# A decoder block on one core: parts of weights' sums one tile later, branch weights asked for ahead of pooling data, a table loaded earlier, and four last products on GpSimd

## The chip, the core and the metric

The kernel runs on one core of one Trainium2 chip. The core has five engines with a queue of instructions each, in order: TensorE (PE in the profile; its loads of stationary operands are listed apart as PEld), VectorE (DVE), ScalarE (ACT), GpSimd (POOL) and SyncE (SP), which here only asks for transfers. Engines wait for each other on semaphores. The metric is device time in microseconds (us), lower is better; it is compared as the median of several runs.

## What is computed

One decoder layer over a sequence of 1024 rows of width 1024, in float32:

```python
h = x
h = h + 0.5 * swiglu(rms_norm(h, ffn1_norm), ffn1_w1, ffn1_w3, ffn1_w2)     # FFN 1, inner width 2816
u = rms_norm(h, mix_norm)
proj = u @ w_in              # q | k | v of 12 heads, pooling input (512 wide), logits of two gates
gates = sigmoid(...)
y_attn = dilated_mixture_attention(q, k, v) @ w_branch_attn                  # 256 -> 1024
y_pool = multiscale_pool(pz, pool_w, pool_scale) @ w_branch_pool             # 512 -> 1024
h = h + (gates[0] * y_attn + gates[1] * y_pool) @ w_out
h = h + 0.5 * swiglu(rms_norm(h, ffn2_norm), ffn2_w1, ffn2_w3, ffn2_w2)     # FFN 2
out = rms_norm(h, final_norm)
```

where `swiglu(x, w1, w3, w2)` is `(silu(x @ w1) * (x @ w3)) @ w2` and `rms_norm` divides each row by the root of its mean square and multiplies by a gain.

## The kernel before

**Products.** Every float32 operand is split into a high part (an ACT copy to the type fp32r) and a low part (the operand less its high part, on DVE or POOL), and a product of two operands is three matmuls: high by high, high by low, low by high. The large products also use a scheme with seven block products in place of eight: 2x2 blocks of weights and of rows are added and subtracted first (tiles whose names begin with `s_` for weights; `t1` to `t4`, `b11`, `b21`, `b22` for rows), and the seven products are made of these sums. `Quad.operand(m)` (from L331) makes the weights' operand of product m: for m = 6 and m = 7 it computes sums on DVE (L345 and L347 for m = 6), then calls `Sevens.split`, which makes the high part on ACT (L303) and the low part on an engine that it is given or that it picks by a counter: every third on DVE, the others on POOL (L306).

**Entries.** Three phases begin with an entry: FFN 1, the input projection ("mix"), and FFN 2. `Entry.run` goes over the last four of the eight tiles of 128 rows, `t` = 4 to 7. For each it normalises the next tile's rows (`squares`, `inverse` with a power on POOL, `scaled` on DVE, L267), forms the row sums in PSUM with transposes on PE (L381, L458), and makes high (ACT, L382 and L398) and low parts (DVE, L385 and L401). In between PE runs two products of the first quads for each tile, and `out` empties their PSUM bank: an ACT activation, L527 in FFN 1 and FFN 2 (tile `y_f`), L1032 in the mix phase (`y_m`). At `t` = 5, behind the rest of the tile, it calls `more(0)`, which makes the operand of the first product of the main loop behind the entry (product 6 of the first quad; the text calls this operand M0); `more(1)` stands in the last tile. The order of the instructions on each engine is the order of these calls: it is written out by hand (`manual_schedule`), no scheduler changes it. Bank after bank is used in turn, so a product waits until the bank that it takes has been emptied.

**Branch data.** The inputs of the branch stage are asked for from SP's queue towards the end of the mix phase. `load_pool` (L1241) loads the pooling rows into tiles that held row sums (`xhi_b_mix`, `xlo_b_mix`, `xhi_t_mix`, `xlo_t_mix`); `load_branch` (L1243) loads the branch weights for one block (`wab`, from the DRAM tensor `late_w`, L1245) and then the gate's values for it (`gb`, L1246); `load_values` (L1234) loads v. A "ring" of tiles for q and k is filled by further DMAs (L1204, L1205) and split (L1213 on ACT, L1214 on POOL). The branch products are `yp` (L1701) and the attention's are `s`, `tp` and `o`. `end_branches` asks for the next block's branch weights when one is done.

**The output projection** (from L1999) is a loop over steps `i`; ACT makes the high part `o_hi` at L1923, PE multiplies at L1940. Behind it, FFN 2's entry uses Silu for the first time since the attention's exponentials, so ACT loads a table of functions (`ACT_TABLE_LOAD`, L531).

**The last stage** is FFN 2's down projection: steps 0 to 41, each with operands `a` (gated values, split into `ahi_f` and `alo_f`, L718 and L722) and `b` (weights, sums at L738, split into `bhi_f`, `blo_f`), with products at L760 and additions into `h_last` at L765. Every fourth low part goes to POOL except in the last two steps. Rows 4 to 7 are finished in two halves of columns: behind the addition of the low half `low_half` (L2101) squares it on ACT, and when the last of the four is done `low_rows` (L2107, L2109) multiplies all four low halves by the final gain on DVE. Behind the addition of a high half come its squares (L2113), the sum (L2117), the power on POOL (L2118), the product of the high half (L2123), the scaling of the low half (L2126) and the two stores.

Of the kernel before, what the change touches and what calls it, by code (L numbers as in the profile page):

```python
# [126 lines left out]
def tile_block(  # L127
# [191 lines left out]
    class Quad:  # L319


        def __init__(self, sv, n):
            self.sv, self.n = sv, n
            self.a = []
            self.bank, self.w = {}, {}

# [3 lines left out]

        def operand(self, m, eng=None):  # L331
            if not self.a or (m not in (1, 2) and len(self.a) == 2):
                self.get()
# [20 lines left out]
            else:  # L354
                src = half_tile("s", f"{n}4")
                ve.tensor_tensor(src, a12, self.s2, op=OP.subtract)
            self.w[m] = self.sv.split(src, f"{n}{m}", eng)

# [44 lines left out]
    class Entry:  # L403
# [18 lines left out]
        def run(self, high, after, first=0):  # L422
# [11 lines left out]
            for t in range(4, NT):  # L434
# [24 lines left out]
                if not last:  # L459
# [13 lines left out]
                    self.out(k)  # L473
                    r4 = fourth()
                    r4.lower()
                else:
# [16 lines left out]
                if t == NT - 3:  # L493
                    self.more(0)

# [349 lines left out]
    def pre_run(sv, todo, first, low):  # L845
        return Entry(sv, [(*((q.A, m, q.a_out), (q.B, m, q.b_out))[k],) for q, m in todo for k in range(2)], low,
                     lambda n: first.A.operand((6, 7)[n]))

# [394 lines left out]
    def load_branch(d):  # L1243
        w, gb = row_part(f"wab{d}"), row(f"gb{d}")
        nc.sync.dma_start(w.rearrange("p (q c) -> p q c", q=2).bitcast(F32), late_w[1 + d][:, :, 256:768])  # L1245
        nc.sync.dma_start(gb, gate_dram[d][:, 1])  # L1246
        pool_in[d] = (w.rearrange("p (q c) -> p q c", q=2), gb)

# [5 lines left out]

    def mix_operand(k):
        if k < len(items):
            q, m = items[k]
            if q == len(mixes):
                mixes.append(Mix(svm, q))
            mixes[q].quad.operand(m, None if k > 1 else gp)  # L1260

# [98 lines left out]
    with tc.manual_schedule():  # L1360
# [4 lines left out]
        for k in range(len(items) + 4):  # L1365
# [27 lines left out]
            if k == len(items) - 12:  # L1393
                later.append([k, first_ring()])
            if k == len(items) - 6:
                load_pool(2, "b11", 0)
                load_pool(3, "b11", 1)
# [3 lines left out]
            if k == len(items) - 4:  # L1401
                load_branch(0)
                load_values(0, row_part)
# [285 lines left out]
    def branch(n):  # L1689

        d, half = divmod(n, 2)
        cols = slice(half * HALF, (half + 1) * HALF)
        w, gb = pool_in[d]
        p = bank("acc", f"yp{n}")
# [14 lines left out]
    def end_branches():  # L1709
        while ends:  # L1710
            n, p = ends.pop(0)
            d, half = divmod(n, 2)
            gb = pool_in[d][1]
            cols = slice(half * HALF, (half + 1) * HALF)
            ve.tensor_tensor(gb[:, cols], p, gb[:, cols], op=OP.mult)
            if half == 1:
                stores.append((by_pool[d], gb))
                del pool_in[d]
                if d + 2 < KT:
                    load_branch(d + 2)  # L1720

    def send():
# [76 lines left out]
    with tc.manual_schedule():  # L1799
        load_ring(uses[1], ring_place(1))  # L1800
        load_branch(1)
        factors = [make_factors(hp, eng) for hp, eng in enumerate((gp, ve))]
        combines = [[combine(hp, half, adds, lower) for half in range(2)]
# [168 lines left out]
    with tc.manual_schedule():  # L1972
# [28 lines left out]
        for i in range(2, STEPS - 4):  # L2001
# [3 lines left out]
            if i in (6, 7):  # L2005
                load_whole(i + 4)
            sum_o(i + 3)
            split_o(i + 2)
# [92 lines left out]
    def low_half(t):  # L2101
# [3 lines left out]
        ends[t] = y, st  # L2105

    def low_rows(t):  # L2107
        y, _ = ends[t]
        ve.tensor_tensor(y[:, LOWS], h[t][:, LOWS], final_gain[:, LOWS], op=OP.mult)  # L2109

# [18 lines left out]
    def after2(m, t):  # L2129
# [3 lines left out]
        elif m == len(DOWN) - 2:  # L2133
            low_half(4 + t)
            if t == 3:
                for u in range(4, NT):
                    low_rows(u)
        elif m == len(DOWN) - 1:
# [103 lines left out]
```

## Time and profile before

| | |
|---|---|
| three runs | 1941.24, 1938.65, 1936.98 us; median 1938.65 us |
| profiled execution | 1938.52 us, of which the span of instructions is 1936.7 us |
| mean granted TensorE clock | 0.995 of full |
| busy: PE / DVE / ACT / POOL | 1900.9 / 1341.3 / 776.9 / 730.0 us |
| DMA traffic | 333.56 MB, mean 172 GB/s |

All times in rows are counted from the start of the span. A row of the timeline gives the start, the busy time, the engine, the line of the kernel, the operation, the output tile and its inputs, the shapes, a count when equal instructions follow each other, and in brackets the idle time of the engine just before it, with what ended it. A row of the list of waits gives total idle time, number of times and the longest one, for a pair of waiting and releasing lines. Matmuls are pipelined: each lasts 389 ns in the trace, but they follow each other more closely than that.

### The profile page before, as it was taken

The numbers are of one execution on the slowest core, as the hardware profiler recorded it, in microseconds if no ns is written. First come the engines' busy times: TensorE is split into PE (matmuls) and PEld (weight loads), VectorE is DVE, ScalarE is ACT, GpSimd is POOL, SyncE is SP. The second block draws the span as 40 slices with busy tenths as digits, with TensorE's granted clock in tenths as the row PEclk, the third lists the DMA queues.
The fourth block names the chain that finished last, engine by engine and source line by source line (L and its number), as shares of the span: only waits on it lengthen the run. The fifth ranks groups of instructions, "written<-read, shape, count | busy, mean of one in ns | idle before, by whom it ended". The sixth has DMA issues, their size and how long they took to land. (4 is left out here: it accounts for less than half of the span.)

```text
span 1936.7 us, 24862 instructions
## 1 busy us (share of the span) xinstructions
PE 1900.9 (98%) x8842; PEld 1567.9 (81%) x8842; DVE 1341.3 (69%) x2015; ACT 776.9 (40%) x1396; POOL 730.0 (38%) x556
## 2 busy tenths in 40 slices
PE   9999999999999999999999999999999999999998
PEld 7788888887888877888877888877888888878886
DVE  6786556657776776667875886878666556577777
ACT  6323333333345542334444763263333333333344
POOL 4333333332222344444544365644333333322132
PEclk9999999999999999999999999999999999999999
DMA  4164222336466626765568997642533223454564
GB/s 186 39 201 153 103 87 104 136 111 209 147 229 216 201 83 224 240 227 179 214 240 297 269 256 260 246 174 87 198 105 128 93 87 104 143 195 146 191 217 163
DMA packets 147436, 333.56 MB, mean 172 GB/s; under 512 B 20208, under 2 KB 40944, under 8 KB 145776
## 3 DMA queue, kind: packets, MB, share of 16 engines
q1 hardware_dynamic: 138096, 307.22, 47.1%
q10 hardware_dynamic: 9216, 24.75, 3.6%
q8 instruction: 70, 1.15, 0.3%
q14 instruction: 54, 0.44, 0.1%
HBM read 229.61 MB, written 102.30 MB: 171 GB/s over the span
## 5 line engine op out<-in xcount | busy, mean ns | idle before, releaser
L760 PE MATMUL d_f<-bhi_f,alo_f 128*128 128x512 f32 x616 | 240.4, 390 | 1.7 <-POOL alo_f L722 1.4
L760 PE MATMUL d_f<-bhi_f,ahi_f 128*128 128x512 f32 x616 | 240.5, 390 | 0.5 <-ACT h L389 0.5
L760 PE MATMUL d_f<-blo_f,ahi_f 128*128 128x512 f32 x616 | 239.7, 389 | 0.0
L722 POOL TENSOR_TENSOR alo_f<-g_f,ahi_f 128x512 fp32r<-128x512 f32 x68 | 96.8, 1440 | 282.7 <-ACT ahi_f L718 276.1
L314 PE MATMUL u_mixm<-xhi_t_mix,wc_mixm 128*128 128x512 f32 x608 | 195.1, 391 | 1.2 <-POOL wc_mixm L306 1.1
L314 PE MATMUL u_mixm<-xhi_b_mix,wc_mixm 128*128 128x512 f32 x456 | 148.9, 393 | 4.8 <-ACT y_m L1032 2.8
L760 PEld LDWEIGHTS d_f<-bhi_f,alo_f 128*128 128x128 f32 x616 | 115.6, 188 | 27.5 <-POOL alo_f L722 2.5
L760 PEld LDWEIGHTS d_f<-bhi_f,ahi_f 128*128 128x128 f32 x616 | 115.6, 188 | 24.6 <-ACT h L389 0.9
L314 PEld LDWEIGHTS u_mixm<-xhi_t_mix,wc_mixm 128*128 128x128 f32 x608 | 113.7, 188 | 26.5 <-POOL wc_mixm L306 3.3
L760 PEld LDWEIGHTS d_f<-blo_f,ahi_f 128*128 128x128 f32 x616 | 115.6, 188 | 23.9
L314 PE MATMUL u_mixm<-xlo_t_mix,wc_mixm 128*128 128x512 f32 x304 | 118.3, 389 | 0.0
L306 POOL TENSOR_TENSOR wc_mixm<-s_mixm,wc_mixm 128x512 fp32r<-128x512 f32 x52 | 75.2, 1447 | 107.7 <-ACT wc_mixm L303 99.7
L314 PEld LDWEIGHTS u_mixm<-xhi_b_mix,wc_mixm 128*128 128x128 f32 x456 | 85.5, 188 | 24.5 <-ACT y_m L1032 3.2
L303 ACT ACTIVATE wc_mixm<-s_mixm 128x512 fp32r<-128x512 f32 x76 | 47.7, 629 | 128.0 <-DVE s_mixm L347 53.5
L314 PE MATMUL u_mixm<-xlo_b_mix,wc_mixm 128*128 128x512 f32 x228 | 88.8, 389 | 0.0
L718 ACT ACTIVATE ahi_f<-g_f 128x1024 fp32r<-128x1024 f32 x84 | 81.8, 974 | 3.2 <-DMA g_f<-gs_f 3.2
L306 POOL TENSOR_TENSOR wc_mixm<-raw,wc_mixm 128x512 fp32r<-128x512 f32 x40 | 57.3, 1434 | 58.3 <-ACT wc_mixm L303 58.2
L1940 PE MATMUL wo<-w_o,o_hi 128*128 128x512 f32 x224 | 69.5, 391 | 0.5 <-ACT h_again L389 0.3
L718 ACT ACTIVATE bhi_f<-s_f2w 128x512 fp32r<-128x512 f32 x55 | 32.8, 627 | 88.5 <-DVE s_f2w L738 80.8
L314 PEld LDWEIGHTS u_mixm<-xlo_t_mix,wc_mixm 128*128 128x128 f32 x304 | 57.1, 188 | 11.8
L718 ACT ACTIVATE bhi_f<-s_f1w 128x512 fp32r<-128x512 f32 x55 | 33.0, 630 | 81.6 <-DVE s_f1w L738 76.7
L722 DVE TENSOR_TENSOR alo_f<-g_f,ahi_f 128x1024 fp32r<-128x1024 f32 (+1 forms) x44 | 52.7, 1198 | 7.3 <-ACT ahi_f L718 7.3
(1330 smaller groups left out, 5098.5 us busy)
## 6 DMA issues: line engine op xcount, KB each, us to landing
g_f<-gs_f SPq DMA_DIRECT2D x70, 512.0 KB, 4.5
gs_f<-y_f SPq DMA_DIRECT2D x88, 256.0 KB, 2.5
raw<-in_w2a_dram SPq DMA_DIRECT2D x35, 512.0 KB, 4.3
raw<-in_w2b_dram SPq DMA_DIRECT2D x35, 512.0 KB, 4.1
gs_f<-gb_f SPq DMA_DIRECT2D x46, 256.0 KB, 2.3
raw<-in_w1a_dram SPq DMA_DIRECT2D x22, 512.0 KB, 4.8
raw<-in_w3a_dram SPq DMA_DIRECT2D x22, 512.0 KB, 6.1
raw<-in_w1b_dram SPq DMA_DIRECT2D x22, 512.0 KB, 4.5
```

The costliest lines, as they stand in the source:

```text
L303: ac.activation(w[:, 0], src, AF.Copy)
L306: eng.tensor_tensor(w[:, 1], src, w[:, 0].bitcast(F32), op=OP.subtract)
L314: pe.matmul(p, a, b, start=(start and k == 0 and q == 0), stop=(k == 3 and q == 2), skip_group_check=not start)
L718: ac.activation(hi[:, c], src, AF.Copy)
L722: eng.tensor_tensor(lo[:, d], src[:, o], hi[:, d].bitcast(F32), op=OP.subtract)
L760: pe.matmul(self.banks[m][t], l, r, start=(first and q == 0), stop=(last and q == 2))
L1940: pe.matmul(banks[m][t], l, r, start=(st == 0 and j == 0 and q == 0), stop=(st == 1 and j == 1 and q == 2))
```

## The change

- **Entries.** `operand` is cut in two. `summed(m)` makes the sums alone (the instructions on DVE), and `operand` calls it and then splits. At `t` = 5 the entry now calls `more(0, True)`, which makes M0's sums only; the split is called at `t` = 6, between the high part of that tile's fourth sum and its low part. All three entries do so.
- **Branch weights.** The gate's load is taken out of `load_branch` into `load_gate`. For the first block the weights are now asked for ahead of the four pooling loads; the gate's values stay where they were. The other blocks keep their order.
- **Gate's table.** In the output projection's loop at `i` = 7 a one-column activation with Silu is added, so that the table is loaded there; the load at the entry of FFN 2 goes.
- **Last products.** Each low half's product with the final gain is issued on POOL (`gp`) right behind that half's squares, in `low_half`; `low_rows` and its loop go.

PE's order of instructions is the same in both kernels.

```diff
@@ Quad
         def operand(self, m, eng=None):
+            self.summed(m)
+            self.w[m] = self.sv.split(self.src.pop(m), f"{self.n}{m}", eng)
+
+        def summed(self, m):
+            if m in self.src:
+                return
             if not self.a or (m not in (1, 2) and len(self.a) == 2):
                 self.get()
...
-            self.w[m] = self.sv.split(src, f"{n}{m}", eng)
+            self.src[m] = src
@@ Entry.run
                     r4 = fourth()
+                    if t == NT - 2:
+                        self.more(0)
                     r4.lower()
...
                 if t == NT - 3:
-                    self.more(0)
+                    self.more(0, True)
@@ pre_run
-                     lambda n: first.A.operand((6, 7)[n]))
+                     lambda n, early=False: (first.A.summed if early else first.A.operand)((6, 7)[n]))
@@ mix_operand
-        mixes[q].quad.operand(m, None if k > 1 else gp)
+            if early:
+                mixes[q].quad.summed(m)
+            else:
+                mixes[q].quad.operand(m, None if k > 1 else gp)
@@ load_branch
+    def load_gate(d):
+        gb = row(f"gb{d}")
         nc.sync.dma_start(gb, gate_dram[d][:, 1])
-        pool_in[d] = (w.rearrange("p (q c) -> p q c", q=2), gb)
+        pool_in[d].append(gb)
@@ the mix phase's last items
             if k == len(items) - 6:
+                load_branch(0)
                 load_pool(2, "b11", 0)
                 load_pool(3, "b11", 1)
             if k == len(items) - 5:
                 load_pool(0, "t2", 0)
                 load_pool(1, "t2", 1)
             if k == len(items) - 4:
-                load_branch(0)
+                load_gate(0)
                 load_values(0, row_part)
@@ the output projection's loop
+            if i == 7:
+                ac.activation(warm, mhalf, AF.Silu)
             sum_o(i + 3)
             split_o(i + 2)
@@ the end
         ac.activation(y[:, LOWS], h[t][:, LOWS], AF.Square, scale=D ** -0.5, accum_out=st[:, 0:1])
         ends[t] = y, st
-
-    def low_rows(t):
-        y, _ = ends[t]
-        ve.tensor_tensor(y[:, LOWS], h[t][:, LOWS], final_gain[:, LOWS], op=OP.mult)
+        gp.tensor_tensor(y[:, LOWS], h[t][:, LOWS], final_gain[:, LOWS], op=OP.mult)
...
             low_half(4 + t)
-            if t == 3:
-                for u in range(4, NT):
-                    low_rows(u)
```

More of the change, by code (lines that the diff above doesn't have):

```diff
@@ L324, in __init__ @@
             self.a = []
-            self.bank, self.w = {}, {}
+            self.bank, self.w, self.src = {}, {}, {}
         def get(self):
@@ L1243, in load_branch @@
     def load_branch(d):
-        w, gb = row_part(f"wab{d}"), row(f"gb{d}")
-        nc.sync.dma_start(w.rearrange("p (q c) -> p q c", q=2).bitcast(F32), late_w[1 + d][:, :, 256:768])
+        w = row_part(f"wab{d}").rearrange("p (q c) -> p q c", q=2)
+        nc.sync.dma_start(w.bitcast(F32), late_w[1 + d][:, :, 256:768])
+        pool_in[d] = [w]
+    def load_gate(d):
+        gb = row(f"gb{d}")
         nc.sync.dma_start(gb, gate_dram[d][:, 1])
-        pool_in[d] = (w.rearrange("p (q c) -> p q c", q=2), gb)
+        pool_in[d].append(gb)
     mix_stack = ExitStack()
@@ L1253, in tile_block, with mix_operand @@
     items = [(q, m) for q in range(len(MIX)) for m in ORDER if q >= AHEAD or m not in (1, 2)]
-    def mix_operand(k):
+    def mix_operand(k, early=False):
         if k < len(items):
@@ L1692, in branch @@
         cols = slice(half * HALF, (half + 1) * HALF)
-        w, gb = pool_in[d]
+        w = pool_in[d][0]
         p = bank("acc", f"yp{n}")
@@ L1720, in end_branches @@
                     load_branch(d + 2)
+                    load_gate(d + 2)
     def send():
@@ L1801, in tile_block @@
         load_branch(1)
+        load_gate(1)
         factors = [make_factors(hp, eng) for hp, eng in enumerate((gp, ve))]
```

## The prediction

> **What bounds the kernel now.** I read the engine table of the page first, then the list of waits of the matrix engine (TensorE, "PE"), then the table of clock windows.
>
> ```profile
> span 1936.7 us, 24862 instructions
> PE 1900.9 (98%) x8842; PEld 1567.9 (81%) x8842; DVE 1341.3 (69%) x2015; ACT 776.9 (40%) x1396; POOL 730.0 (38%) x556
> ```
>
> TensorE is idle for 1936.7 − 1900.9 = 35.8 us of the whole span. Nothing in the change removes a matmul, so it can only win a part of these 35.8 us, or shorten stretches that ran at half clock. The list of waits says where they are (columns: who waited, for whom, us in total, times, longest):
>
> ```profile
> PE yp L1701 <- DMA wab<-late_w: 3.3, 1, 3.3
> PE u_f12a L314 <- ACT y_f L527: 3.3, 1, 3.3
> PE u_mixm L314 <- ACT y_m L1032: 2.8, 1, 2.8
> PE u_f21a L314 <- ACT y_f L527: 2.3, 1, 2.3
> PE x_t L381 <- POOL s_f2t L430: 1.2, 1, 1.2
> PE x_t L381 <- POOL s_mixt L430: 0.9, 1, 0.9
> PE x_b L381 <- DVE xlo_t_mix L401: 0.6, 1, 0.6
> ```
>
> These seven, 14.4 us, are the places that the first three parts touch. The next view has one row for each clock window (start and end; then its length, busy us of PE, PEld, DVE, ACT, POOL; the granted clock; the DMA share; GB/s):
>
> ```profile
> 48.75:52.17 3.42, 1.14 (x6) 0.60 (x4) 2.30 (x5) 2.31 (x7) 1.46 (x2) 1.00 0.01 2
> 52.17:55.58 3.41, 2.43 (x6) 1.92 (x7) 3.41 (x5) 1.58 (x4) 3.41 (x3) 0.50 0.00 0
> 55.58:58.99 3.41, 3.41 (x11) 2.63 (x10) 2.50 (x4) 1.54 (x3) 1.60 (x2) 0.50 0.45 154
> 687.04:690.46 3.42, 1.52 (x7) 0.94 (x5) 2.29 (x5) 2.27 (x5) 1.56 (x2) 1.00 0.01 2
> 690.46:693.87 3.41, 2.53 (x10) 1.91 (x11) 3.41 (x5) 1.58 (x4) 3.41 (x3) 1.00 0.00 0
> ```
>
> A window in which PE was busy 1.14 of 3.42 us is followed by two at clock 0.50; one with 1.52 of 3.42 is followed by full clock. So a gap costs its own length and, if its phase is bad, a slow stretch.
>
> **Part A, the three entries.** In the last tile but one of each phase's entry, the high copy of M0 (a sum of weights, L303 on ScalarE, "ACT") moves from ahead of the next tile's rows to behind them, and with it its low part. The sums themselves (L345, L347 on VectorE, "DVE") stay. Rows of the mix entry, the FFN-1 entry and the FFN-2 entry, by engine:
>
> ```profile
> 687.40 0.69 DVE L347 TENSOR_TENSOR s_mixm<-s_mixm,raw 128x512 f32<-128x512 f32 x1
> 688.08 0.69 DVE L460 TENSOR_TENSOR x_b<-x_b,h 128x512 f32<-128x512 f32 x1
> 688.19 0.63 ACT L303 ACTIVATE wc_mixm<-s_mixm 128x512 fp32r<-128x512 f32 x1 [2.14 <-DVE nst L263]
> 690.68 0.61 ACT L1032 ACTIVATE y_m<-u_mixm 128x512 f32<-128x512 f32 x1
> 691.06 1.93 DVE L267 SCALAR_TENSOR_TENSOR hn_mix<-h,nst,gain_mix 128x1024 f32<-128x1024 f32 x1
> 696.36 0.69 DVE L401 TENSOR_TENSOR xlo_t_mix<-x_t,xhi_t_mix 128x512 fp32r<-128x512 f32 x1 [0.66 <-ACT xhi_t_mix L398]
> 58.16 0.69 DVE L401 TENSOR_TENSOR xlo_t_f<-x_t,xhi_t_f 128x512 fp32r<-128x512 f32 x1 [0.66 <-ACT xhi_t_f L398]
> 1300.05 1.28 ACT L531 ACT_TABLE_LOAD   x1
> 1300.30 1.27 DVE L267 SCALAR_TENSOR_TENSOR hn_f<-h_again,nst,gain_ffn 128x1024 f32<-128x1024 f32 x1
> 1315.82 0.69 DVE L401 TENSOR_TENSOR xlo_t_f<-x_t,xhi_t_f 128x512 fp32r<-128x512 f32 x1 [0.66 <-ACT xhi_t_f L398]
> ```
>
> The gap ahead of u_mixm ends with the ACT copy that empties the bank (L1032). Ahead of it on ACT stands the M0 copy, but the row copy that follows also needs DVE's subtraction L460, done at 688.08 + 0.69 = 688.77. So taking 0.63 us of ACT away does not bring the whole 2.78 us: the row copy L398 can start near 688.8 instead of 689.72, and the emptying near 689.8 instead of 690.68. I take 0.9 us at the gap, and 1.9 us of idle remain. The second effect is on DVE: L267, the next tile's scaled rows, starts about 0.9 us earlier, and takes 1.93 us here but 1.27 us in the row of 1300.30; the long one lies where POOL subtracts M0's low part (POOL was busy 3.41 of 3.41 us in the window from 690.46). With that work gone the next rows are ready about 0.9 + 0.65 = 1.5 us earlier, and with them the whole chain of the last tile down to its last low part (L401 at 696.36, for which PE waits the 0.58 us): 1.5 us in the mix entry (0.9 to 1.6).
>
> In FFN-1 the chain moves by the same 1.5 us, so that its L401 ends near 57.3 instead of 58.85. What it is worth depends on the clock. PE worked on until 59.58 there because it ran at half clock up to 58.99. If the shortened gap (2.4 us) triggers the two slow windows again, the gain is about 0.5 us; if not, 59.58 − 57.3, about 2.2. I take the middle, 1.4. By the Trainium skill (TensorE: Matmul & The Clock Gate, section "What's actually happening") the clock halves after at least one idle window of about 3.4 us, which neither the gap of 3.26 nor one of 2.4 us fills; the row of 48.75 differs, since one third busy was enough to halve it, and the measurement decides. By the page alone the gain here would be the upper end.
>
> In FFN-2 the low part of M0 changes engine: in the built order it stands on DVE, not POOL, between the last tile's subtraction L445 and the low part L401 at 1315.82. That puts about 0.7 us (the 0.69 of a DVE row) and a wait for ACT's copy of M0 into the very chain that is shortened by 1.2 to 1.5 us. I take 0.5 (0 to 1.6). The table load of 1.28 us leaves this entry too (part C); it lies ahead of the 1.16 us wait for s_f2t, which should vanish, but PE then only arrives earlier at the same DVE chain, and its gap at u_f21a does not shrink (2.3 to 2.6). The two changes share the one 0.5.
>
> **Part B, branch weights.** One DMA, wab, moves ahead of four pooling loads on SP's queue; the gate's load stays.
>
> ```profile
> 1062.20 1.35 PE L1701 MATMUL yp<-xhi_b_mix,wab 128*128 128x512 f32 x3 [3.30 <-DMA wab<-late_w]
> 1048.61 0.61 SPq L1245 DMA_DIRECT2D wab<-late_w  x1
> 1041.20 0.34 SPq L1241 DMA_DIRECT2D xhi_b_mix<-pool  x1
> 1044.29 0.43 SPq L1241 DMA_DIRECT2D xlo_t_mix<-pool  x1
> xlo_t_mix<-pool SPq DMA_DIRECT2D x1, 1024.0 KB, 10.9
> GB/s 249 205 224 199 161 85 0 0 175 197 415 459 404 426 426 426 426 426 437 415 339 240 208 295 421 426 399 415 410 382 273 281 401 404 399 415 426 421 404 415
> 1073.13 0.63 ACT L1213 ACTIVATE xlo_b_mix<-xhi_b_mix 128x512 fp32r<-128x512 f32 x1 [0.66 <-DMA xhi_b_mix<-qk]
> ```
>
> wab waits at PE's gap of 3.30 us. The transfer rates (one number for each 0.75 us from 1036 to 1066) show the engines idle near 1040.5 to 1042, just ahead of the pools; 512 KB at 426 GB/s take 1.2 us and fit. So the gap goes, and PE is not held at 1058.9. What is late next: the ring data, for which ACT still waits at 1073.13 (0.66 us) and on which the stage's later products hang. Transfers run near 400 GB/s from 1043 on, so the ring data can land only as much earlier as bytes left the queue: those 1.2 us. A full gain of 3.3 us would need the later work to come 3.3 us earlier as well. I take 1.2 (0.6 to 3.3). The four pools can start no later for it: the first was issued only at 1041.20, after SP had waited.
>
> **Part C, the table load.** It moves into the output-projection loop at its eighth step, where ACT waits for PE:
>
> ```profile
> 1243.45 1.06 ACT L1923 ACTIVATE o_hi<-o_sum 128x1024 fp32r<-128x1024 f32 x1 [4.38 <-PE wo L1940]
> ```
>
> 4.38 us of idle hide 1.28 us and one tiny activation: cost 0. Without that cover it would push the next o_hi copy by at most 1.3 us.
>
> **Part D, the last products.** Four products of 128x512 go from DVE to POOL, and earlier: the first ahead of POOL's last two alo subtractions, three behind them.
>
> ```profile
> 1922.61 2.49 DVE L2109 TENSOR_TENSOR n<-h_last,gain_final 128x512 f32<-128x512 f32 x4
> 1925.01 0.68 DVE L765 SCALAR_TENSOR_TENSOR h_last<-d_f,h_last 128x512 f32<-128x512 f32 x1
> 1926.46 0.39 PE L760 MATMUL d_f<-bhi_f,alo_f 128*128 128x512 f32 x1
> 1928.50 0.39 PE L760 MATMUL d_f<-bhi_f,alo_f 128*128 128x512 f32 x1
> 1929.87 0.69 DVE L765 SCALAR_TENSOR_TENSOR h_last<-d_f,h_last 128x512 f32<-128x512 f32 x1
> L738 DVE TENSOR_TENSOR s_f2w<-raw,raw x9: 674/686/1784, 1898.5 to 1918.7; 128x512 f32<-128x512 f32 x9
> 1920.81 0.69 DVE L722 TENSOR_TENSOR alo_f<-g_f,ahi_f 128x512 fp32r<-128x512 f32 x1
> 1911.20 3.00 POOL L722 TENSOR_TENSOR alo_f<-g_f,ahi_f 128x512 fp32r<-128x512 f32 x2 [6.43 <-ACT ahi_f L718]
> ```
>
> Today the four products hold DVE until 1925.10, and every later addition L765 is pushed; the last starts at 1929.87, although PE ended at 1928.50 + 0.39 = 1928.89. With DVE free the last could start at 1928.95: a gain of 0.9. Against it: DVE's subtraction L738 takes 686 ns in the middle and 1784 at most, and the long ones fall where POOL works on alo (1912 to 1914). Products of about 1.5 us on POOL (two alo subtractions took 3.00), two of them among DVE's preparation of the last two steps, would stretch two or three DVE operations by 1.1 us each; some of it fits in DVE's idle time. The last alo ends at 1921.50. Each of the last four tiles takes PE 2.04 us (1926.46 to 1928.50), so the first takes that alo three times 2.04 us before the last, at 1928.50 − 6.12 = 1922.38, a slack of 0.9. With about 2 us more on DVE, PE stops for about 1 us, and the end comes out nearly where it was: gain 0.1 (−0.5 to 0.9). The rule that speaks against this part is in the Trainium skill (SBUF — State Buffer, section "Who interferes with whom"): a VectorE instruction with two SBUF inputs and a GpSimd instruction that reads SBUF block each other for a whole instruction. The L738 row agrees, 686 against 1784 ns.
>
> **The sum.** 1.4 + 1.5 + 0.5 + 1.2 + 0 + 0.1 = 4.7 us. The profiled execution took 1938.52 us (0.13 below the median of the three runs shown, 1938.65): 1938.5 − 4.7 = 1933.8. A measurement can tell about 0.2%, 3.9 us, from no change; the forecast is faster by a little more.
>
> **The rivals.**
> 1. Most is eaten: A's chain is bound elsewhere, or slow clock windows come back; B gives 0.6, D −0.5, A 0.5 + 0.9 + 0: together 1.5, 1937.0. For it: only parts of each gap go even by my own count. Against it: the M0 copy stands plainly ahead of the emptying in three entries. If M0's copy were not on the path at all, the whole change would not do what it says there, and only B + D, 1.3 us, would remain: 1937.2, the same case.
> 2. Everything binds as first read: A 2.2 + 1.6 + 1.6, B 3.3, D 0.9: 9.6 us, 1928.9. For it: the list of waits names exactly these causes. Against it: the ring wait at 1073.13 and the DVE and POOL overlap.
> 3. Slower: wab now heads SP's queue, and a wait of its own there would hold the four pools. They land up to 1044.29 + 10.9 = 1055.2, 3.7 us ahead of the gap's start at 1058.9. Held by 3.7 us plus the 3.3 us of today's gap plus the other parts' 3.5, 10.5 us in all, nothing is won; from 14.4 the kernel is slower by 0.2%, near 1942.5. Against it: in the built order wab waits for an old transfer and an old POOL operation, both ahead of the qk_in load of 1037.2, and the DMA engines go idle behind that.
>
> **How the numbers follow.** The forecast has 0.52, rival 1 0.28, rival 2 0.12, rival 3 with other ways to lose 0.08. Faster by over 0.2% is rival 2 and nearly all of the forecast's case: 0.61; within it 0.30 (rival 1 and a rest); slower 0.09. The range reaches from 1930.5, part of the way to rival 2, to 1937.2, the end of rival 1; the forecast's own is 1932 to 1935.
>
> **What would show it.** Right: gaps of about 2.4, 1.9 and 2.5 us ahead of u_f12a, u_mixm and u_f21a; L267 at 1.3 us there; no wait for s_mixt or s_f2t; wab landing before 1043 and no gap at L1701, with ACT's ring wait kept; the table load near 1240; DVE's L738 or L722 stretched beside POOL's products, and PE stopping up to 1 us near 1922. Wrong: the pools landing after 1059, M0's low part holding L401 by over 1.5 us in FFN-2, or PE running on at 1922 and the last addition at its end (D then 0.9).

## The result and the profile after

The changed kernel takes 1932.75 us, median of 15 runs (1931.47 to 1935.34), against 1936.98 us of the kernel before in 15 runs beside it. The ratio is 0.9976, 95% interval 0.9968 to 0.9984: about 4.6 us faster (3.1 to 6.2); the two medians differ by 4.2. The forecast was 4.7. The profiled execution took 1933.69 us.

The engine table of the page, after:

```profile
span 1931.8 us, 24861 instructions
PE 1900.9 (98%) x8842; PEld 1567.5 (81%) x8842; DVE 1341.1 (69%) x2012; ACT 776.9 (40%) x1397; POOL 732.4 (38%) x559
```

PE's busy time is the same to a tenth, so the whole 4.9 us between the two spans is idle time of PE: 30.9 us in place of 35.8. The waits of PE, after (who waited, for whom, us in total, times, longest):

```profile
PE tp L1630 <- ACT e L1610: 2.6, 2, 2.5
PE u_f12a L314 <- ACT y_f L535: 2.3, 1, 2.3
PE u_f21a L314 <- ACT y_f L535: 2.3, 1, 2.3
...
PE u_mixm L314 <- ACT y_m L1040: 1.9, 1, 1.9
...
PE d_f L768 <- ACT ahi_f L726: 0.7, 1, 0.7
...
PE x_b L387 <- DVE xlo_t_f L407: 0.6, 1, 0.6
```

The 3.3 us for `wab` are gone, but a wait of 2.5 us for the exponentials `e` is new; the three gaps of the entries (u_f12a, u_mixm, u_f21a) are 2.3, 1.9 and 2.3 us, where the prediction said 2.4, 1.9 and 2.5; a stop of 0.7 us at step 41 of the last stage is new.

PE runs the same 8842 matmuls in the same order in both kernels, so the start of one and the same matmul can be compared in the two traces, and the time from one such matmul to another is the length of that stretch. The boundaries, by their starts in the kernel before, are 40.11, 80.06, 680.01, 730.05, 1057.10, 1185.92, 1295.92, 1339.98, 1920.11 and 1928.50 us (the last matmul):

| stretch | before, us | after, us | won | forecast |
|---|---|---|---|---|
| FFN 1 entry (40.11 to 80.06) | 39.95 | 37.91 | 2.0 | 1.4 |
| mix entry (680.01 to 730.05) | 50.04 | 48.44 | 1.6 | 1.5 |
| branches (1057.10 to 1185.92) | 128.82 | 128.63 | 0.2 | 1.2 |
| FFN 2 entry (1295.92 to 1339.98) | 44.07 | 43.38 | 0.7 | 0.5 |
| last 8 us of PE (1920.11 to 1928.50) | 8.39 | 10.01 | −1.6 | about −1 |
| the tail: last matmul's start to the end of the span | 8.25 | 7.10 | 1.15 | 0.9 (0.1 for both) |
| all the rest | 1657.2 | 1656.4 | 0.9 | 0 |

So the sum came out right while its terms did not: the entries gave more, the branches hardly anything.

Two steps of the mix entry, after, on ACT and DVE:

```profile
687.34 0.60 ACT L1040 ACTIVATE y_m<-u_mixm 128x512 f32<-128x512 f32 x1
...
687.61 1.27 DVE L267 SCALAR_TENSOR_TENSOR hn_mix<-h,nst,gain_mix 128x1024 f32<-128x1024 f32 x1
...
692.25 0.69 DVE L407 TENSOR_TENSOR xlo_t_mix<-x_t,xhi_t_mix 128x512 fp32r<-128x512 f32 x1 [0.66 <-ACT xhi_t_mix L404]
```

This trace runs 2.44 us ahead when PE reaches the gap. With that added, the emptying L1040 starts at 689.78 (689.8 was forecast, 690.68 was before), the scaled rows take 1.27 us in place of 1.93, and the last low part starts at 694.69 in place of 696.36, 1.67 us earlier (1.5 was forecast).

### The profile page after: what moved, and what is told of

Read it like the earlier page. It is cut to its first block, busy times and chain, and to the rows that moved or that the text cites. A ratio compares the mean times of both kernels' runs of the same rounds, so it can differ in the third digit from the quotient of the medians.

```text
span 1931.8 us, 24861 instructions
## 1 busy us (share of the span) xinstructions
PE 1900.9 (98%) x8842; PEld 1567.5 (81%) x8842; DVE 1341.1 (69%) x2012; ACT 776.9 (40%) x1397; POOL 732.4 (38%) x559
## 3 DMA queue, kind: packets, MB, share of 16 engines
q8 instruction: 70, 1.15, 0.2%
## 5 line engine op out<-in xcount | busy, mean ns | idle before, releaser
L306 POOL TENSOR_TENSOR wc_mixm<-s_mixm,wc_mixm 128x512 fp32r<-128x512 f32 x52 | 75.2, 1447 | 102.8 <-ACT wc_mixm L303 87.9
```

What stands on the lines that cost most here:

```text
L306: eng.tensor_tensor(w[:, 1], src, w[:, 0].bitcast(F32), op=OP.subtract)
```

## The experiments

All were timed beside the kernel before on the same chip; 0.9976 is the ratio to compare with, and a second set of runs of the changed kernel gave 0.9977 (0.9968 to 0.9985, median 1933.26). Intervals of single kernels are near ±0.0009, ±1.7 us, so terms below 2 us are read from the stretches.

A stretch also depends on how many windows at half clock fell into it. Part A stands whole in ten traces: FFN 1's entry takes 37.4 to 37.5 us in the six of them with no such window there and 37.9 in the four with one, the mix entry 48.4 in five with none and 48.8 in five with one. FFN 2's entry takes 43.4 in the changed kernel's traces with one and in two others without (the fills and the exponentials below). Below, a stretch is compared with one of as many slow windows where there is one.

### The four parts, each undone

**Part A undone**, the rest kept:

```diff
                     r4 = fourth()
-                    if t == NT - 2:
-                        self.more(0)
                     r4.lower()
...
-                    self.more(0, True)
+                    self.more(0)
```

> The changed kernel with part A alone undone: M0's sums and split stand again behind tile 5 in all three entries. The account of the two traces so far gives part A 2.0 us in FFN 1, 1.6 in the mix phase and up to 0.7 in FFN 2: this kernel is then 3.6 to 4.3 us slower than the changed one, close to the kernel before (within 1.5 us of it), and the gaps ahead of u_f12a and u_mixm are back at 3.3 and 2.8 us. The prediction's own terms give 3.4 us. A rival, that the three spans differ by chance of the clock windows and not by the order of the instructions, gives less than 2 us, and gaps of the old length without later low parts.

Measured: 1937.72 us, ratio 1.0003 (0.9995 to 1.0012). Entries: 40.02, 50.95 and 44.80 us. The gaps returned; waits of PE:

```profile
PE u_f12a L314 <- ACT y_f L533: 3.3, 1, 3.3
PE u_f21a L314 <- ACT y_f L533: 3.2, 1, 3.2
PE u_mixm L314 <- ACT y_m L1038: 2.8, 1, 2.8
```

Without part A nothing is left of the gain: 5 us of difference between the ratios, more than the 3.6 to 4.3 expected. By the stretches it is 6.0 us against the changed kernel, where the kernel before has 4.3. Apart from the table load in FFN 2's, the entries have the same order of instructions in these two; what differs is the clock, which ran through two half-clock windows here both in the mix entry and in FFN 2's, where the kernel before had none and one. Within the noise part A is the whole gain.

**Part B undone:**

```diff
             if k == len(items) - 6:
-                load_branch(0)
                 load_pool(2, "b11", 0)
...
+                load_branch(0)
                 load_gate(0)
```

> The changed kernel with part B alone undone: the branch weights are asked for behind the pooling loads again. Theory from the traces: the wait of 3.3 us for the weights was exchanged for a wait of 2.5 us for the exponentials behind ACT's ring copy, and a half-clock window goes with either; undone costs 0 to 0.6 us. The prediction's term is 1.2 us. The rival that the whole gap was won gives 3.3 us. In the trace the interval from the first s of the branch stage (L1583 or its counterpart) to the waits for o near 1141 is to be 87.0 us by the theory, 88.2 by the prediction, 90.3 by the rival.

Measured: 1934.95 us, ratio 0.9986 (0.9977 to 0.9995); the branch stretch takes 129.1 us. The wait is back:

```profile
PE yp L1717 <- DMA wab<-late_w: 3.5, 1, 3.5
```

By the ratios part B is worth 1.9 us, but the two intervals overlap. By the stretch it is 0.4 against the changed kernel's trace. Over a shorter interval, from the first s to the matmuls s that start at 1140.26 in the changed kernel, it is 87.9 us against 87.1, between the 0 to 0.6 expected and the prediction's 1.2. The stretch is not the same in every execution: in the eleven traces of kernels that ask for `wab` early and leave the order of ACT there alone it took 126.8 to 131.7 us (median 128.2), without it 128.8 and 129.1. A part of that is the clock: 126.8 to 127.8 us in three traces with no half-clock window there, 127.6 to 128.9 (mean 128.4) in seven with one, 131.7 with two. The kernel before had one at 128.8, this kernel two. Whether B is worth nothing or 2 us isn't settled; that the whole 3.3 us of the wait were won is out.

**Part C undone:**

```diff
-            if i == 7:
-                ac.activation(warm, mhalf, AF.Silu)
```

> The changed kernel without the early Silu: the table load stands again in FFN 2's entry. The prediction says 0 beyond what it shares with M0's order (the same DVE chain ends the entry either way): below 0.3 us. The rival is that the load's 1.28 us are most of what FFN 2's entry won (0.7 us in the trace): then this kernel is 0.7 to 1.2 us slower, and the wait of about 1.2 us for s_f2t is back while the gap at u_f21a stays at 2.3.

Measured: 1933.84 us, ratio 0.9982 (0.9973 to 0.9991); FFN 2's entry takes 43.51 us against 43.38. The waits of this kernel:

```profile
PE x_b L387 <- DVE xlo_t_f L407: 2.2, 2, 1.7
...
PE x_t L387 <- POOL s_f2t L436: 1.5, 2, 1.2
PE u_f21a L314 <- ACT y_f L535: 1.3, 1, 1.3
```

The 1.2 us for s_f2t are back, and the wait at u_f21a is 1.0 shorter for it; in this trace no slow clock window fell there, so PE was earlier at the last x_b and waited 1.7 us for its low part in place of 0.6. The same DVE chain ends the entry either way: two other traces without a slow window there, with the table loaded early, show that wait of 1.7 us too, and the entry takes 43.37. The rival had the gap at u_f21a at 2.3; it fell. Part C moved 0.1 us.

**Part D undone** (the products on DVE behind the fourth low half, as in the kernel before):

```diff
-        gp.tensor_tensor(y[:, LOWS], h[t][:, LOWS], final_gain[:, LOWS], op=OP.mult)
...
             low_half(4 + t)
+            if t == 3:
+                for u in range(4, NT):
+                    low_rows(u)
```

> The changed kernel with part D alone undone: the four products on DVE behind the last low half. Theory from the traces: part D cost PE 1.6 us ahead of its last 27 matmuls and gave back 1.1 us behind the last one, so this kernel is about 0.4 us faster than the changed one, with no stop of PE in the last 15 us and 7.8 us from the last matmul to the end of the span. The prediction's term gives 0.1 us slower; the rival that the products on DVE were simply in the way gives 0.9 us slower.

Measured: 1933.40 us, ratio 0.9982 (0.9973 to 0.9991); last 8 us of PE 8.39, tail 8.58. PE's stop is gone and the tail is long again, longer than the 7.8 expected. Both together take 16.97 us here, 16.64 in the kernel before; with part D 17.11, 16.95 in its second trace. Part D is worth 0 within 0.5 us, and its two effects are both there, larger than forecast.

### Where part D loses, and a better place

The theory is that POOL and DVE block each other when both read from SBUF. The changed kernel's POOL, DVE, ACT and PE rows:

```profile
1910.31 1.74 POOL L2126 TENSOR_TENSOR n<-h_last,gain_final 128x512 f32<-128x512 f32 x1
...
1910.82 2.38 DVE L730 TENSOR_TENSOR blo_f<-s_f2w,bhi_f 128x512 fp32r<-128x512 f32 x2
...
1917.74 0.68 DVE L730 TENSOR_TENSOR alo_f<-g_f,ahi_f 128x512 fp32r<-128x512 f32 x1
...
1916.78 0.61 ACT L726 ACTIVATE ahi_f<-g_f 128x512 fp32r<-128x512 f32 x1
...
1917.45 0.50 PE L768 MATMUL d_f<-bhi_f,ahi_f 128*128 128x512 f32 x1 [0.74 <-ACT ahi_f L726]
1917.87 0.51 PE L768 MATMUL d_f<-blo_f,ahi_f 128*128 128x512 f32 x1
1918.47 0.50 PE L768 MATMUL d_f<-bhi_f,alo_f 128*128 128x512 f32 x1
```

Beside a product of 1.74 us on POOL, two DVE operations take 2.38 us, of which one alone takes 0.69 (the row at 1920.81 of the kernel before). The delay reaches PE through ACT's copy and again through blo and alo: each of three matmuls waits for its operand. The last of them, which takes alo, starts 1.47 us late against PE's own work before the stop; the 0.15 us that are left of the 1.6 are lost in the matmuls just behind.

**Fills in place of products:**

```diff
-        gp.tensor_tensor(y[:, LOWS], h[t][:, LOWS], final_gain[:, LOWS], op=OP.mult)
+        gp.memset(y[:, LOWS], 0.0)
```

> The changed kernel with the four products on POOL replaced by four fills of the same tiles with zero, which write as much and read nothing; so it leaves the low halves' products out. Theory: POOL and DVE block each other when both read two tiles of SBUF; with fills, DVE's operations of steps 39 to 41 beside them go back to 0.68 us (those beside POOL's alo subtractions stay at 1.78), PE does not stop at step 41, and the last stage takes 8.4 to 8.7 us of PE instead of 10.0. Rival: any POOL operation on those tiles, or the mere order on POOL's queue (alo behind a product), delays DVE: 9.6 us or more.

Measured: 1930.41 us in one run, with no interval, of a kernel that leaves the low halves' products out; last 8 us of PE 8.39, tail 7.10. The first of POOL's four operations and DVE's sum that starts 0.3 us behind it, in the changed kernel and, below the dots, here:

```profile
1903.54 1.51 POOL L2126 TENSOR_TENSOR n<-h_last,gain_final 128x512 f32<-128x512 f32 x1 [3.72 <-ACT n L2124]
1903.82 1.78 DVE L746 TENSOR_TENSOR s_f2w<-raw,raw 128x512 f32<-128x512 f32 x1
...
1901.82 0.53 POOL L2126 MEMSET n<- 128x512 f32 x1 [3.70 <-ACT n L2124]
1902.12 0.68 DVE L746 TENSOR_TENSOR s_f2w<-raw,raw 128x512 f32<-128x512 f32 x1
```

Beside the product the sum takes 1.78 us and ends 0.55 us behind it, as if it had begun only when POOL was done. Beside the fill it takes its ordinary 0.68 us and ends 0.45 us behind it; a sum held up to the fill's end would have come 0.1 us later. PE does not stop, and the place on POOL's queue is the same, so the order isn't what hurts. A fill is shorter than a product as well, 0.53 against 1.29 to 1.74 us, so of the 1.6 us that PE wins this run doesn't part reading from length; that the sum is not held at all beside the fill speaks for reading, by one overlap and 0.1 us. With this reading the Trainium skill agrees (SBUF — State Buffer, section "Who interferes with whom"): a VectorE instruction with two SBUF inputs contends with a GpSimd instruction that reads SBUF, not with one that only writes it.

**One product earlier on DVE:**

```diff
-        gp.tensor_tensor(y[:, LOWS], h[t][:, LOWS], final_gain[:, LOWS], op=OP.mult)
...
             low_half(4 + t)
+            if t == 2:
+                low_rows(4)
+            if t == 3:
+                for u in range(5, NT):
+                    low_rows(u)
```

> The changed kernel with its four last products on DVE again, one of them behind the third low half and three behind the fourth (the kernel before had all four behind the fourth). Theory: what cost PE 1.6 us in part D was that POOL and DVE block each other, not the earlier place. One DVE product of 0.68 us fits into the slack of 0.9 us, so PE does not stop, the last stage takes 8.4 us of PE as before, and with the first addition 0.6 us earlier the tail falls from 8.3 to 7.6 us; 0.8 to 1.2 us faster than the changed kernel. Rival: any delay of DVE's preparation reaches PE, which stops for about 0.6 us, and the sum is the same as in the kernel before.

Measured: 1933.74 us, ratio 0.9982 (0.9973 to 0.9991); last 8 us 8.63, tail 8.33. PE stopped for 0.24 us, where none was expected, and the theory failed in its second half, the earlier first addition; the two together, 16.96 us, are those of the kernel with part D undone (16.97): no gain, as the rival had it. The first addition and the last matmul:

```profile
1924.18 0.68 DVE L773 SCALAR_TENSOR_TENSOR h_last<-d_f,h_last 128x512 f32<-128x512 f32 x1
...
1927.59 0.39 PE L768 MATMUL d_f<-bhi_f,alo_f 128*128 128x512 f32 x1
```

It starts 3.41 us ahead of the last matmul; in the kernel before it was 1928.50 − 1925.01 = 3.49. The product that was brought forward only pushed DVE's own later work by its 0.6 us: DVE's idle time there is a wait for ACT, which waits for DVE, and moves along. Nothing was taken off DVE ahead of the first addition.

**Products spread on DVE, and M0's low part on POOL in FFN 2.** First the low part alone:

```diff
-    lambda n, early=False: (first.A.summed if early else first.A.operand)((6, 7)[n]))
+    lambda n, early=False: first.A.summed(6) if early else first.A.operand((6, 7)[n], (gp, None)[n]))
```

> The changed kernel with M0's low part on POOL in FFN 2's entry too, as it is in the other two. The prediction charged about 0.7 us to its place on DVE ahead of the last tile's low part: PE's wait of 0.63 us at x_b then goes, and FFN 2's entry falls from 43.4 to 42.7 us; 0.7 us in all, below what the times can tell. Rival: PE is bound by its gap of 2.35 us at u_f21a alone and x_b is not on the path: 0.

Measured: 1932.56 us, ratio 0.9977 (0.9968 to 0.9986), which can't be told from the changed kernel; FFN 2's entry takes 42.65 us against 43.38. PE's wait for the last low part, 0.63 us, is gone. The 0.7 us that the prediction charged to DVE there are shown by the stretch.

Then with the products spread:

```diff
-        gp.tensor_tensor(y[:, LOWS], h[t][:, LOWS], final_gain[:, LOWS], op=OP.mult)
...
             low_half(4 + t)
+            if t == 3:
+                low_rows(4)
+                low_rows(5)
         elif m == len(DOWN) - 1:
             high_half(4 + t)
+            if t in (0, 2):
+                low_rows(6 + t // 2)
```

> The changed kernel with two edits. M0's low part is on POOL in FFN 2's entry (0.7 us, as measured). The four last products are on DVE again but spread: two behind the fourth low half, one behind the first high half's squares and one behind the third's, where DVE waited for ACT. Theory: the tail behind the last matmul is set by the first addition, from which tile to tile DVE, ACT and POOL need about 1.55 to 1.76 us in turn; with two products of 0.6 us less ahead of it, the first addition comes 1.2 us earlier, the last near the end of PE, and PE is not disturbed: last stage 8.4, tail 7.2 to 7.6 us, together 15.6 to 16.0 against 17.1; with the low part 1.8 to 2.2 us faster than the changed kernel. Rival: the products, wherever they stand on DVE, delay the last addition as much as before: tail 8.2, and only 1.1 us in all.

Measured: 1930.15 us (1929.01 to 1931.58), ratio 0.9964 (0.9951 to 0.9978): the lowest median of the kernels that compute the whole layer, 3.1 us below the changed kernel in the runs beside it, though the two intervals still overlap (five runs here). Last 8 us of PE 8.39, tail 7.11, together 15.50 against 17.11; FFN 2's entry 42.66; that is 2.3 us by the stretches, and the branch stretch happened to take 126.8 us in this trace, with no half-clock window there. DVE and PE:

```profile
1914.23 1.28 DVE L2129 TENSOR_TENSOR n<-h_last,gain_final 128x512 f32<-128x512 f32 x2
1915.43 0.68 DVE L773 SCALAR_TENSOR_TENSOR h_last<-d_f,h_last 128x512 f32<-128x512 f32 x1
1916.03 0.68 DVE L2129 TENSOR_TENSOR n<-h_last,gain_final 128x512 f32<-128x512 f32 x1
...
1920.55 0.69 DVE L773 SCALAR_TENSOR_TENSOR h_last<-d_f,h_last 128x512 f32<-128x512 f32 x1
...
1920.12 0.39 PE L768 MATMUL d_f<-bhi_f,alo_f 128*128 128x512 f32 x1
```

The first addition now starts 1920.12 − 1915.43 = 4.69 us ahead of the last matmul, and the last addition at 1920.55, at the end of that matmul. All four products are on DVE, so they were never too much for it; two of them stood at a place where the tail waited.

### Part A taken apart

**High copy back behind tile 5, low part in tile 6:**

```diff
+        def high_part(self, m, eng=None):
+            self.summed(m)
+            self.w[m], self.held[m] = self.sv.split(self.src.pop(m), f"{self.n}{m}", eng, True)
...
-    lambda n, early=False: (first.A.summed if early else first.A.operand)((6, 7)[n]))
+    lambda n, early=False: first.A.high_part(6, gp) if early else first.A.operand((6, 7)[n]))
...
```

(`split` with `True` makes the high part and hands back the subtraction, which `operand` runs later; the mix entry likewise.)

> Part A cut in two: M0's high copy is back behind tile 5, as in the kernel before, and only its low part (on POOL in all three entries) is made in tile 6. Theory: two effects add up. The gaps at u_f12a, u_mixm and u_f21a return (3.3, 2.8 and 2.3 or more) because ACT's copy is ahead of the bank's emptying again, which costs 0.9 us in each entry against the changed kernel; the scaled rows L267 stay at 1.27 us because POOL does not subtract beside them, which keeps 0.65 us in each against the kernel before. Entries (FFN 1, mix): 38.3 to 39.3 and 49.3 to 49.6 us. Rival: the low part on POOL is all of it: entries as in the changed kernel (37.4 to 37.9 and 48.4). Other rival: the high copy is all: as before (40.0 and 50.0 to 50.9).

Measured: 1936.65 us, ratio 0.9996 (0.9987 to 1.0005). Entries 38.24, 49.71 and 43.61 us. A wait and the scaled rows of this kernel:

```profile
PE u_mixm L320 <- ACT y_m L1053: 2.8, 1, 2.8
...
689.17 1.27 DVE L267 SCALAR_TENSOR_TENSOR hn_mix<-h,nst,gain_mix 128x1024 f32<-128x1024 f32 x1
```

Both effects are there and come apart: the gaps are back in full (3.3, 2.8 and 3.3 us), L267 stays at 1.27. The entries lie 0.1 us outside the expected ranges. This trace had no slow window in FFN 1's entry and one in each of the other two. Against traces with as many, the later high copy is worth 38.24 − 37.45 = 0.8 us in FFN 1, 49.71 − 48.8 = 0.9 in the mix entry, and 43.61 − 42.65 = 1.0 in FFN 2 (against the kernel with the low part on POOL there), close to the 0.9 of the theory. The later low part can be estimated in the mix entry: 50.04 without a slow window before, 49.71 − 0.4 here, so 0.7 us, where 0.65 was said. In FFN 1 the kernel before has two slow windows, which no trace with the later low part has, so its share there is mixed with the clock's.

**The sums later, too:**

```diff
                     r4 = fourth()
-                    if t == NT - 2:
-                        self.more(0)
                     r4.lower()
+                    if t == NT - 2:
+                        self.more(0)
...
-                if t == NT - 3:
-                    self.more(0, True)
...
```

(M0's low part in FFN 2 goes to POOL with the edit shown above.)

> The changed kernel with M0's two sums moved as well, behind the low part of tile 6's fourth row sum, and its low part on POOL in all three entries. Theory of the prediction: the idle that is left at u_f12a, u_mixm and u_f21a (2.35, 1.9 and 2.35 us) hangs on DVE, where the two sums of 0.7 us stand ahead of the subtraction: the gaps fall to 0.9 to 1.1 us and each entry is 0.5 to 1.4 us shorter, 2 to 4 us in all. Rival: DVE's work in the last tile is the bound behind it, so that the sums only push that and M0's low part, and PE waits as long at u_f10a or x_b: no gain, or up to 1 us lost in each entry.

Measured: 1938.07 us, ratio 1.0004 (0.9995 to 1.0013): all of the gain lost. Waits:

```profile
PE u_f10a L314 <- DVE xlo_t_f L391: 1.9, 1, 1.9
PE u_mixm L314 <- DVE xlo_t_mix L391: 1.9, 1, 1.9
...
PE u_f12a L314 <- ACT y_f L533: 1.5, 1, 1.5
```

The gaps fell, to 1.5, 0.5 and 1.0 us, so what is left of them does hang on DVE's two sums. But DVE has no room for 1.4 us in the last tiles: PE waits 1.9 us at the main loop's first product in each phase, and the entries take 40.2, 50.9 and 44.7 us. The rival was right, and the loss is larger than it said: 1.3 to 2.4 us in each entry against the changed kernel.

### Part B: what is late next

**Exponentials ahead of the ring copies, in the third pair:**

```diff
+            ring_now = i > 1 and u + 1 < len(uses)
-            if i > 1 and u + 1 < len(uses):
+            if ring_now and q != 2:
                 split_ring(uses[u + 1], i - 2)
                 split_ring(uses[u + 1], i)
             end_branches()
             exponents(2 * q)
             exponents(2 * q + 1)
+            if ring_now and q == 2:
+                split_ring(uses[u + 1], i - 2)
+                split_ring(uses[u + 1], i)
```

> The changed kernel with one reordering on ACT: in the third pair of attention blocks the exponentials go ahead of the two copies of ring data. Theory: part B won almost nothing because ACT's copy waits for ring data that are bound by the DMA engines, and the exponentials, and then PE's transposes tp, stand behind it. Then PE's wait of 2.5 us for e goes, and the stretch from the first s to 1090 falls from about 33.2 us to 31 to 32; the whole is 1 to 2 us faster than the changed kernel. Rival: the ring data are needed just as soon by PE's own scores, so the wait only moves to the next s (on POOL's low part or ACT's copy), the stretch stays within 0.5 us and so does the time.

The order in the changed kernel, on ACT and PE, and its transfer rates (0.75 us each from 1039 to 1069):

```profile
1068.07 0.63 ACT L1221 ACTIVATE xlo_b_mix<-xhi_b_mix 128x512 fp32r<-128x512 f32 x1 [2.10 <-DMA xhi_b_mix<-rot]
1068.61 0.49 ACT L1610 ACTIVATE e<-e,stats 128x256 f32<-128x256 f32 x1
...
1069.25 1.01 PE L1630 MATMUL tp<-ident,e 128*128 128x128 f32 x4 [2.46 <-ACT e L1610]
...
GB/s 393 404 339 448 415 437 415 459 393 415 382 240 208 229 371 410 410 415 421 437 421 404 415 426 360 262 393 432 412 404 358 197 145 240 90 153 251 57 254 412
```

Measured: 1932.63 us, ratio 0.9976 (0.9967 to 0.9985), no different from the changed kernel. The first 33.2 us of the stretch (up to a matmul tp that starts at 1090.16 in the kernel before) fell to 30.3, and the rest gave it back: 129.4 us in all. PE's waits in this kernel:

```profile
PE yp L1717 <- DMA wab<-late_w: 1.4, 1, 1.4
```

ACT's ring copy ahead of the exponentials was the wait, as thought, but behind it stands the next transfer, the second block's `wab`. What sets the length of the whole stretch wasn't isolated. That ring data are bound by full DMA engines, as the theory had it, is not what the row of rates shows: in the slices from 1062.25 to 1068.25, in which ACT waited, they moved 57 to 254 GB/s. The account of part B below has what the ring waited for.

**The changed kernel once more:**

> The changed kernel once more, to have it beside the others on one chip and a second trace of it: 4.2 to 5 us faster than the kernel before; the last stage 10.0 us of PE and a tail of 7.1; the branch stretch up to 1090 within 1 us of 33.4, which says how far single traces of that stretch can be compared.

Measured: 1933.26 us, ratio 0.9977. Entries 37.46, 48.83 and 43.36 us, branches 128.47, last 8 us 9.85, tail 7.10. The first 33.2 us of the branch stretch took 33.0, within the 1 us expected.

## Why the prediction was right, point by point

- **A, the gaps.** Right: 0.9 us of each gap went in FFN 1 and the mix phase and 1.9 to 2.4 remained, since DVE's sums stand ahead of the subtraction. The later sums show it from the other side: with them moved, the gaps fell. The wait for s_mixt was to go; 0.3 of 0.9 us stayed.
- **A, the scaled rows.** The size was right, 1.27 us in place of 1.93, and the run with the high copy back shows it as an effect of its own. The reading was not: L267 does not lie beside M0's low part. POOL in the mix entry, before and, below the dots, after:

```profile
688.90 1.27 POOL L306 TENSOR_TENSOR wc_mixm<-s_mixm,wc_mixm 128x512 fp32r<-128x512 f32 x1 [3.79 <-ACT wc_mixm L303]
690.64 3.51 POOL L306 TENSOR_TENSOR wc_mixm<-raw,wc_mixm 128x512 fp32r<-128x512 f32 x2
...
686.33 1.26 POOL L306 TENSOR_TENSOR wc_mixm<-raw,wc_mixm 128x512 fp32r<-128x512 f32 x1
688.54 1.50 POOL L306 TENSOR_TENSOR wc_mixm<-raw,wc_mixm 128x512 fp32r<-128x512 f32 x1 [0.95 <-ACT wc_mixm L303]
```

  M0's subtraction (the one from s_mixm) was over at 690.17, ahead of the 691.06 of L267. It had pushed two other weights' subtractions behind it, and L267 started inside the first of these. Without it the first ends at 687.59, just ahead of L267 at 687.61, and the second starts only inside L267, which then keeps its 1.27 us.
- **A, the clock in FFN 1.** Too low, 1.4 for 2.0. The forecast was the middle between two slow windows again (0.5) and none (2.2). The gap did halve the clock, but for one window, and the entry won 2.0 us; in the repeat, without a slow window there, 2.5. What failed is the weight on two windows: no trace with part A whole has them, so "about 0.5 us" stands untested.
- **A, FFN 2.** Right within 0.2: 0.7 for 0.5. The low part on DVE costs 0.73 us, 0.7 was said. That the table load shares the DVE chain was right: 0.1.
- **B.** Wrong in size: 1.2 forecast, 0.2 to 0.4 by the stretch, not settled by the times. `wab` came early as forecast (the rows below: issued at 1033.3 and landed 5.1 us later, 16 us before PE's first yp at 1054.5). ACT's wait for the ring was named, but two steps failed. The prediction left out that the exponentials stand behind the ring copy in ACT's queue, so PE sat idle for 2.46 us at tp. And the ring data did not land as much earlier as bytes left the queue: the copy at 1073.13 came at 1068.07 with a trace 4.30 us ahead, so 0.76 us earlier and not 1.2, because its transfers were asked for late. The changed kernel's issue of `wab`; its SP's wait for the gate's transfer, and the one before; SP's request for a piece of the ring behind that wait, and how long such pieces took to land:

```profile
L1253 SPq DMA_DIRECT2D wab<-late_w x1: 607/607/607, 1033.3 to 1033.3; - x1
...
DMA to landing us min/median/max: 5.1/5.1/5.1
...
SPq L1213 <- DMA gate<-y_m: 8.0, 4, 5.5
...
SPq L1204 <- DMA gate<-y_m: 7.6, 4, 4.6
...
1062.53 0.30 SPq L1213 DMA_DIRECT2D xhi_b_mix<-rot  x1
...
DMA to landing us min/median/max: 2.0/2.7/2.9
```

  SP sat for 5.5 us until a transfer of the gate's values had landed; then it asked for the rest of the ring, and the pieces of `rot`, for which ACT waits, landed within 3 us. The gate's own two transfers, 512 KB each, took 8.6 us to land, at rates near 400 GB/s: there the engines come in. The kernel before has that wait too, with 4.6 us at most, so an earlier `wab` brings the ring little. This is read from the traces; no run moved the ring's requests.

- **C.** Right: nothing beyond what it shares.
- **D.** Both effects right in kind. "PE stops for about 1 us" came out as 1.6. The slack of alo was as said, 1922.38 − 1921.50 = 0.88; the term that was mis-sized is the delay on DVE, "about 2 us": against the matmul at 1920.11 and its counterpart at 1914.73, alo ended 1.39 us behind before and 1918.42 − 1914.73 = 3.69 after, 2.3 us later. ACT's high copy and blo were late too, but alo came last and alone sets what its matmul loses. The tail won 1.15 where 0.9 was said. Net −0.5 in this pair of traces, and about −0.2 over all traces with and without it; forecast 0.1.

The total, 4.7 for a measured 4.6 (3.1 to 6.2), owes its closeness to luck, errors of both signs that cancel: A about 0.9 too low, B about 1 too high, D 0.6 too high, and 0.9 us of small differences outside the stretches.

## What to carry to other kernels

When a wait names one late transfer or one engine, look in the queue of each engine behind it for what would be late next, and ask when each transfer is asked for: of the 3.3 us for `wab`, most came back as 2.5 us for the exponentials, behind a copy whose data had been asked for late. An instruction moved to another engine costs what it does to its neighbours there: POOL had room for the products here, but they stretched DVE's operations. Here the work at the end was best spread into the idle spots of the engine that already has it, two behind the last low half and one each behind later squares, and not in a block ahead of the first step that the tail waits for.

## What the runs showed that I had not expected

- The clock halves after windows that are far from idle. The changed kernel's repeat in the mix entry (columns as in the prediction):

```profile
685.53:688.95 3.41, 1.54 (x7) 1.02 (x6) 3.34 (x5) 2.09 (x4) 2.45 (x3) 1.00 0.00 0
688.95:692.36 3.41, 3.41 (x10) 2.55 (x10) 2.64 (x5) 2.08 (x4) 2.07 (x2) 0.50 0.55 156
```

  PE was busy 1.54 of 3.41 us, and the next window was slow; in the kernel before 1.52 us were followed by full clock, so busy time alone doesn't decide. In the run with the exponentials first, a window with PE busy 2.49 of 3.41 us was followed by a slow one:

```profile
1133.23:1136.64 3.41, 2.49 (x19) 2.05 (x20) 2.71 (x14) 2.72 (x11) 2.83 (x7) 1.00 0.83 271
1136.65:1140.06 3.41, 3.41 (x12) 2.83 (x12) 3.11 (x13) 2.85 (x11) 3.41 (x4) 0.50 1.36 162
```

  One slow window makes the FFN 1 and mix entries about 0.4 us longer (48.83 with, 48.44 without, in two traces of the changed kernel); in FFN 2's entry, which DVE's chain ends, it costs nothing.
- In the one overlap shown above a fill on POOL beside a DVE sum from SBUF cost DVE nothing (0.68 us); products on POOL do (1.78 at most).
- The branch stretch varied by 5 us between traces (126.8 to 131.7) in the eleven traces with `wab` early, more than the change there could have brought.
